# Two held-back steps instead of four, query weights a stage sooner, attention tiles in another order, conditioning sums spread out

## The chip, the cores and the metric

The kernel runs on one core of one Trainium2 chip. The core has a matrix engine (PE in the profile; PEld are its weight loads, which overlap the matmuls), VectorE (DVE), ScalarE (ACT), GpSimd (POOL) and a queue engine (SP) that issues most of the loads from memory; ScalarE issues the stores and a few loads. The metric is the device time of one execution in microseconds (us), the median of several runs.

## The reference

The reference is a two-layer encoder trunk in float32 on one sequence of 1024 rows of width 1024, steered by a conditioning vector `c`.

```
mod = silu(c) @ ada_w[l] + ada_b[l]                  # six vectors of 1024 per layer
h = modulate(rmsnorm(x, g0), shift_m, scale_m)
y = short_conv_mixer(h)                              # layer 0: w_in (1024x3072), 3 taps, gates, w_out
y = mla_mixer(h)                                     # layer 1: 8 heads, low-rank queries, shared low-rank keys and values
x = x + gate_m * rmsnorm(y, g1)
h = modulate(rmsnorm(x, g2), shift_f, scale_f)
y = square(relu(h @ w_up)) @ w_down                  # 1024x4096 and 4096x1024
x = x + gate_f * rmsnorm(y, g3)
```

Before layer 1 the shared keys and values are computed from `x` through a latent of 256 channels, with a norm and a conditioning of their own; queries go through a latent of 384 channels with weights `q_a_w`, then `q_b_w`. Attention is causal by chunks of 64 rows.

## The kernel before, in words

Every matrix product is done in a split form: each float32 operand is written as a high part (a copy by ScalarE) and a low part (a subtraction by VectorE), and three matmuls replace one (`mm`, L155 to L157; `split_w`, L159 to L161). The large products use a seven-product scheme over 2x2 blocks, so that PE does seven block products instead of eight; the sums of blocks are VectorE's.

Loads go through `raw_tile` (L91): four buffers of 512 KB each, shared by all weights, by activations read back from memory and by conditioning matrices. A load is issued when the buffer that it takes has been read.

The order of the instructions on each engine is set by a planner from the dependences and from estimated times; it keeps program order as a priority. Inside `pinned` (L101) the order of the program is kept: for all engines but SP, or for those named.

The stages in order, as far as they are touched:

- *Conditioning.* Each conditioning vector is a list of small steps (`ada_fm`, `ada_bc`, L205 and L241): eight 512 KB loads, each followed by one multiply-add of 128x1024 on VectorE (L187), then a reduction (L218) and a few very small matmuls (L227). The steps wait in a list `bg`, and `run_bg(n)` puts the next n into the program at that point. Each `one(k)` issues the load for k + 1 and then adds k.
- *Convolution* (`conv_phase`): the input projection runs as nine pair jobs (`all_pairs`), each calling `between`, which runs three background steps. `run_bg(99)` stands at its end.
- *Output projections* (`down`, L788): the convolution's and the attention's. Eight rows of 128 channels in chunks of 2, 2 and 4 rows. `fill_row` (L640) splits a row of weights and a row of activations into one slot (`slots_of`); for each chunk PE runs over eight row tiles. In the last chunk each tile goes through `Seam.tile` (L315): square sum on ScalarE, scaling and residual on VectorE, another square sum, the store, and the next norm on ScalarE.
- *Up projection* (`mlp_up`): pairs 0 to 15. `between(i)` runs background steps.
- *Down projection* (`down_pairs`, L646): seven products of eight steps each, in the order 0, 1, 3, 6, 4, 5, 2. A step loads its operands, splits them into rings (four for the one operand, three, later four, for the other) and does 24 matmuls for four row tiles. The last four steps of the last product (`LATE = 4`) are not done in line: their operands are kept, and after the loop each of the four tiles of the second half gets its 24 remaining matmuls and then its `Seam.tile`. The norms of the first half's tiles run meanwhile (`half0`), and `h_steps` (L412) transposes the normed rows for the next stage: a group is four transposes on PE, two outputs on ScalarE (L424) and one subtraction on VectorE (L430). In the first layer `preps` loads and splits the three query weight tiles, after steps 2, 4 and 6 of the last product.
- *Latents* (`first_latents`, L559): three times 24 matmuls; during the third, the transposes of the second half's rows.
- *Attention*: tiles come from the pool `at`, in the order in which they are first asked for. The arena of slots for the output projection is laid over this pool afterwards; a slot can be filled once every tile under it has been read.

Of the kernel before, what the change touches and what calls it, by code (L numbers as in the profile page):

```python
# [17 lines left out]
P = 128  # L18
# [19 lines left out]
PAIRS = D_FF // P // 2  # L38
LATE = 4
RMS = math.sqrt(D)  # L40
# [9 lines left out]
def trunk_kernel(ctx: ExitStack, tc: tile.TileContext, x, c, ada_w, ada_b, norm_g, conv_in_w, conv_w,  # L50
# [300 lines left out]
    def quarter_steps(ys, key, ops):  # L351


        s1, sh = vtile["s" + key], vtile["h" + key]
        kept = [quarter_tile(kk, F32) for kk in range(4)]
        pairs = {}

        def turned(dst, k, half):
            p_ = tp_ps()
            for t in range(4):  # L360
                nc.tensor.transpose(p_[:, t * P:(t + 1) * P], ys[half * 4 + t][:, k * P:(k + 1) * P], ident)
            nc.scalar.activation(dst, p_, AF.Identity, scale=s1[:, k:k + 1], bias=sh[:, k:k + 1])
# [283 lines left out]
    def down_pairs(ys, wd, before, seam, key=None, preps=()):  # L646

        r1, r2, r3, l1 = pool("r1", "right"), pool("r2", "right"), pool("r3", "right"), pool("l1")
        n = PAIRS // 2
        w4 = wd.rearrange("(q two p) d -> p q two d", two=2, p=P)  # L650
        ws = {b: {} for b in ("11", "12", "22")}
# [46 lines left out]
        def half0(i):  # L698

            if i in (3, 5, 7, 9):  # L700
                seam.ahead = 1
                seam.tile((i - 3) // 2, None, [])
            with pinned():
                if i in (0, 2, 4, 6, 8, 10):
                    seam.flush()
                    early(i // 2)
                if i > 10:
                    seam.back()
                    seam.front(steps, 1)
            if i in (n + 2, n + 4, n + 6) and preps:  # L710
                preps.pop(0)(up)

        with pinned([mybir.EngineType.SP]):
            for which, one, more, b, make, done in (
# [11 lines left out]
                if which == 5:  # L726
                    l1.release()
                    xp = pool("xp")
                elif which == 2:
                    r3.release()  # L730
                    r4 = pool("r4", "right")
                    pbs.append(ring(r4))
                    if key:
                        h0 = pool("h0")
                        dst = tuple(h0.tile([P, KD, HALF], F32R, name=nm("h0")) for _ in range(2))
                        up = pool("up")
                        steps = h_steps(tp, ys, 0, key, dst, bank_ps, True)
                for i in range(n):
# [19 lines left out]
                    if which == 5:  # L758
                        half0(i)
                    if which == 2 and i >= n - LATE:  # L760
                        half0(n + i)
                        late.append((pa, pb))
                        continue
# [9 lines left out]
            for t in range(4):  # L773
                with pinned([mybir.EngineType.PE]):
                    for j, (pa, pb) in enumerate(late):
                        products(banks_[t], t, pa, pb, False, j == LATE - 1, True)
                    seam.tile(4 + t, lambda: done(t, banks_[t]), [])
# [10 lines left out]
    def down(slots, sizes, wd, src_fn, ys, seam, steps, per_chunk_bg, before_last=None):  # L788
# [4 lines left out]
        for n_rows in sizes:  # L793
# [9 lines left out]
            for t in range(NT):  # L803
# [10 lines left out]
                else:  # L814
                    nc.vector.tensor_tensor(ys[t], ys[t], p_, op=ALU.add)

    def from_dram(hd):
# [23 lines left out]
    def conv_phase():  # L841
# [213 lines left out]
        for step in all_pairs(up, ops, [job for j in range(1, 4) for job in triple(j)])[::-1]:  # L1055
            step()
        run_bg(99)
        up.release()
# [24 lines left out]
    def mlp_up(l, up, ops, firsts, per_pair_bg):  # L1083
# [32 lines left out]
        def between(i):  # L1116
            flush()
            if i >= AHEAD:
                run_bg(per_pair_bg)
# [128 lines left out]

    h1.release()
    up.release()  # L1250
    h0.release()
    xp.release()
# [9 lines left out]
    def part(pl, tag, bufs, shape):  # L1262
        return tuple(pl.tile(shape, F32R, tag=tag + "hl"[i], name=nm(tag), bufs=bufs) for i in range(2))

    def kv_weights(raw):
# [219 lines left out]
    bg += ada_bc(ad, "g1f", w1, 5 * D, ada_b[1:2, 5 * D:6 * D], norm_g[1, 3:4, :])  # L1485
    last = mlp_up(1, up, hs, firsts, 1)
    ys = [row_tile() for _ in range(NT)]
# [43 lines left out]
```

## Time and profile before

| | us |
|---|---|
| median of 3 runs | 2171.38 (2169.84 to 2172.59) |
| the profiled execution: its time | 2170.84 |
| its span, from first to last instruction | 2169.1 |
| PE busy in it | 2068.5 (95%) |
| VectorE busy | 1542.0 (71%) |
| ScalarE busy | 1083.7 (50%) |
| mean clock granted to PE | 0.988 of full speed |
| read from memory, written | 258.94 MB, 83.89 MB |

A profile line of the timeline reads: start, duration, engine, line of the kernel, operation, output and inputs, shapes, count, and in brackets how long the engine was idle before and what ended that. "PE" lines give each matmul's latency, which overlaps the next; the pace is read from a long run of them. A window line gives, for a stretch, the busy time of each engine with the instructions in it, then the granted clock of PE, the busy share of the transfer engines and the rate in GB/s.

### The profile page before, as it was taken

To read this page: it belongs to the slowest core of one execution; us is meant where nothing else is said; L and a number is where in the kernel's file an instruction comes from. 1 tells how busy PE (TensorE), PEld (TensorE's weight loads), DVE (VectorE), ACT (ScalarE), POOL (GpSimd) and SP (SyncE) were. 2 spreads that over 40 slices of the span, in tenths; PEclk is the share of its full clock that TensorE was granted. 3 is DMA by queue.
4 is the path that set the end of the run, shared out by engine and by line. 5 is a ranking of instruction groups with operands and counts; after the bars stand their busy time and mean duration, and the time that the engine had idled before them with its cause. 6 is when DMAs were issued, how large, how long until landed. Compare 5 with 4: busy or idle time off the path is not lost.

```text
span 2169.1 us, 25064 instructions
## 1 busy us (share of the span) xinstructions
PE 2068.5 (95%) x9438; PEld 1690.3 (78%) x9438; DVE 1542.0 (71%) x2087; ACT 1083.7 (50%) x1533; POOL 5.3 (0%) x13
## 2 busy tenths in 40 slices
PE   4999999889999999998999999989899999999998
PEld 3788878678888788886777888878678888788886
DVE  6877866877655669877688887665876665566576
ACT  4533353735554444455665655564744454544443
POOL 0000000000000000000000000000000000000000
PEclk9999999999999999998999999999999999999999
DMA  7344464256444889546213331043255553774355
GB/s 227 112 140 146 137 200 143 85 195 206 152 146 141 285 289 327 191 152 216 87 50 123 94 104 36 29 156 127 77 194 185 189 170 121 268 247 164 96 174 172
DMA packets 251023, 344.47 MB, mean 159 GB/s; under 512 B 19253, under 2 KB 142482, under 8 KB 250902
## 3 DMA queue, kind: packets, MB, share of 16 engines
q1 hardware_dynamic: 208408, 252.50, 37.0%
q10 hardware_dynamic: 42494, 90.38, 11.2%
q8 instruction: 74, 1.21, 0.2%
q14 instruction: 47, 0.39, 0.1%
HBM read 258.94 MB, written 83.89 MB: 158 GB/s over the span
## 4 chain that ended last, share of the span: by engine, by line
PE 75%; DVE 13%; ACT 6%; DMA 4%; issue 2%; ACTq 0%; SPq 0%; DVEq 0%
PE one L157 41%; PE mm L157 19%; PE tp L157 7%; PE big L157 4%; PE big L1334 2%; ACT junk L272 2%; DMA raw<-in_ada_w_dram 1%; DVE y L328 1%; PE tp L1360 1%; DVE raw L329 1%; DVE acc L187 1%; DMA raw<-ha 1%; DVE av L889 1%; ACT z L1192 1%; DMA aw<-in_ada_w_dram 1%
## 5 line engine op out<-in xcount | busy, mean ns | idle before, releaser
L157 PE MATMUL one<-slot,uphi 128*128 128x512 f32 x1224 | 377.8, 390 | 0.0
L157 PEld LDWEIGHTS one<-slot,uphi 128*128 128x128 f32 x1224 | 230.4, 188 | 48.1 <-issue 0.5
L157 PE MATMUL one<-ring,ring 128*128 128x512 f32 x1152 | 263.0, 390 | 2.3 <-DVE ring L161 2.3
L157 PEld LDWEIGHTS one<-ring,ring 128*128 128x128 f32 x1152 | 215.8, 188 | 48.4 <-ACT ring L160 3.1
L157 PE MATMUL one<-slot,uplo 128*128 128x512 f32 x612 | 240.9, 394 | 8.6 <-DVE y L516 3.8
L161 DVE TENSOR_TENSOR uplo<-raw,uphi 128x1024 fp32r<-128x1024 f32 x127 | 153.2, 1221 | 131.2 <-ACT uphi L160 131.2
L161 DVE TENSOR_TENSOR ring<-raw,ring 128x1024 fp32r<-128x1024 f32 x144 | 174.2, 1219 | 55.8 <-ACT ring L160 55.4
L160 ACT ACTIVATE ring<-raw 128x1024 fp32r<-128x1024 f32 x144 | 149.5, 1051 | 110.6 <-DMA raw<-ha 60.2
L157 PE MATMUL mm<-ring,ring 128*128 128x512 f32 x768 | 189.3, 396 | 7.0 <-DVE ring L161 7.0
L160 ACT ACTIVATE uphi<-raw 128x1024 fp32r<-128x1024 f32 x127 | 134.5, 1060 | 113.0 <-PE one L157 82.1
L157 PE MATMUL big<-slot 128*128 128x512 f32 x768 | 178.9, 393 | 5.3 <-DVE slot L161 4.5
L157 PE MATMUL tp<-ring,ring 128*128 128x512 f32 x768 | 183.9, 389 | 0.0
L160 ACT ACTIVATE ring<-w 128x1024 fp32r<-128x1024 f32 x80 | 84.8, 1060 | 186.0 <-PE tp L157 95.7
L157 PEld LDWEIGHTS mm<-ring,ring 128*128 128x128 f32 x768 | 146.3, 191 | 39.8 <-DVE ring L161 6.0
L157 PEld LDWEIGHTS big<-slot 128*128 128x128 f32 x768 | 144.5, 189 | 36.5 <-DVE slot L161 5.2
L157 PEld LDWEIGHTS tp<-ring,ring 128*128 128x128 f32 x768 | 144.0, 188 | 29.8
L161 DVE TENSOR_TENSOR ring<-w,ring 128x1024 fp32r<-128x1024 f32 x80 | 97.7, 1221 | 88.5 <-ACT ring L160 87.9
L157 PEld LDWEIGHTS one<-slot,uplo 128*128 128x128 f32 x612 | 115.3, 188 | 36.8 <-DVE y L516 5.5
L187 DVE SCALAR_TENSOR_TENSOR acc<-raw,csil,acc 128x1024 f32<-128x1024 f32 x88 | 112.5, 1279 | 27.6 <-DMA raw<-in_ada_w_dram 23.1
L514 ACT ACTIVATE y<-one 128x512 f32<-128x512 f32 x66 | 39.0, 592 | 165.0 <-PE one L157 111.3
L157 PE MATMUL mm<-slot,uphi 128*128 128x512 f32 x344 | 108.7, 398 | 9.5 <-DVE slot L386 9.3
L157 PE MATMUL one<-slot,s 128*128 128x512 f32 x468 | 114.5, 394 | 3.3 <-DVE s L161 3.3
(268 smaller groups left out, 3464.9 us busy)
## 6 DMA issues: line engine op xcount, KB each, us to landing
ha<-y ACTq DMA_DIRECT2D x224, 256.0 KB, 4.1
raw<-ha SPq DMA_DIRECT2D x112, 512.0 KB, 4.0
raw<-in_ada_w_dram SPq DMA_DIRECT2D x80, 512.0 KB, 4.0
raw<-in_mlp_up_w_dram SPq DMA_DIRECT2D x70, 512.0 KB, 4.2
w<-in_mlp_down_w_dram SPq DMA_DIRECT2D x48, 512.0 KB, 6.8
raw<-in_mlp_down_w_dram SPq DMA_DIRECT2D x32, 512.0 KB, 4.7
raw<-in_conv_in_w_dram SPq DMA_DIRECT2D x18, 512.0 KB, 4.0
xs<-raw ACTq DMA_DIRECT2D x18, 512.0 KB, 2.6
```

Of the source, the lines that this page charges most:

```text
L157: nc.tensor.matmul(out_, lhs[a], rhs[b], start=first and i == 0, stop=last and i == 2, skip_group_check=more)
L160: nc.scalar.activation(hi, src, AF.Copy)
L161: nc.vector.tensor_tensor(lo, src, hi.bitcast(F32), op=ALU.subtract)
L187: nc.vector.scalar_tensor_tensor(acc, raw, s, acc, op0=ALU.mult, op1=ALU.add)
L272: nc.scalar.activation(junk, src, AF.Square, accum_out=ss)
L328: nc.vector.scalar_tensor_tensor(y, y, rroot(ss), self.gmb, op0=ALU.mult, op1=ALU.mult)
L329: nc.vector.tensor_tensor(xr, xr, y, op=ALU.add)
L514: nc.scalar.activation(dst, x_, AF.Copy)
L889: nc.vector.scalar_tensor_tensor(acc, raw[:, i, :], csil[:, i:i + 1], acc, op0=ALU.mult, op1=ALU.add)
L1192: nc.scalar.activation(y[32 * i:32 * i + 32, :], p_[32 * j:32 * j + 32, :], AF.Copy, scale=scale)
L1334: nc.tensor.matmul(o_, a, m_, start=j == 0, stop=j == 4)
L1360: nc.tensor.transpose(p_[:, c:c + P], pts[4 * hf + i][:, j * P:(j + 1) * P], ident)
```

## The change

Five edits, none of which changes what is computed:

1. `LATE = 4` becomes `n_late`, two in the first layer's down projection, four in the second's. The transposed groups come two a step, after steps 3, 4 and 5 of the last product, and none after steps 6 and 7; two remain for the tiles after the loop.
2. The query weights are loaded and split in steps 0 to 2 of the product before (`which == 5`). For this the pool `up` is made before `h0` and lies where the weights of block "12" were, beside `xp`.
3. The call that drains the conditioning steps at the end of the convolution is gone; in `down` one step follows each tile of the chunks before the last. The two vectors are looked up where they are used.
4. In the up projections the steps begin at pair 8 instead of pair 4; in the second layer they come two a pair instead of one.
5. In the pool `at` the tiles of key weights, query weights and one rotary scratch tile are asked for first, so that they lie lowest, after the sine table.

```diff
-LATE = 4
@@ quarter_steps
-        s1, sh = vtile["s" + key], vtile["h" + key]
         def turned(dst, k, half):
+            s1, sh = vtile["s" + key], vtile["h" + key]
@@ down_pairs
+        n_late = 2 if key else 4
...
                 if i > 10:
                     seam.back()
-                    seam.front(steps, 1)
-            if i in (n + 2, n + 4, n + 6) and preps:
+                    seam.front(steps, 2 if i < 2 * n - n_late else 0)
+            if i < 3 and preps:
                 preps.pop(0)(up)
...
                 if which == 5:
                     l1.release()
                     xp = pool("xp")
+                    if key:
+                        up = pool("up")
...
                         dst = tuple(h0.tile([P, KD, HALF], F32R, name=nm("h0")) for _ in range(2))
-                        up = pool("up")
...
-                    if which == 2 and i >= n - LATE:
+                    if which == 2 and i >= n - n_late:
...
-                        products(banks_[t], t, pa, pb, False, j == LATE - 1, True)
+                        products(banks_[t], t, pa, pb, False, j == n_late - 1, True)
@@ down
                     nc.vector.tensor_tensor(ys[t], ys[t], p_, op=ALU.add)
+                if f < nf:
+                    run_bg(1)
@@ conv_phase
-        run_bg(99)
@@ mlp_up
-            if i >= AHEAD:
+            if i >= 2 * AHEAD:
                 run_bg(per_pair_bg)
@@ latents and attention
     h1.release()
+    h0.release()
     up.release()
-    h0.release()
...
+    for shape, tags in (([P, 2, HALF], ("kwh", "kwl")), ([P, 3, 256], ("qwh", "qwl")), ([P, HALF], ("zb",))):
+        for tag in tags:
+            at.tile(shape, F32 if tag == "zb" else F32R, tag=tag, name=nm(tag), bufs=1)
...
-    last = mlp_up(1, up, hs, firsts, 1)
+    last = mlp_up(1, up, hs, firsts, 2)
```

## The prediction

> **What bounds the kernel now.** I read four views in this order: the page's totals, the waits of PE (the matrix engine), a table of short windows around the long waits with the clock granted to PE, and the timeline there, engine by engine.
>
> ```profile
> span 2169.1 us, 25064 instructions
> PE 2068.5 (95%) x9438; PEld 1690.3 (78%) x9438; DVE 1542.0 (71%) x2087; ACT 1083.7 (50%) x1533; POOL 5.3 (0%) x13
> ```
>
> PE is busy for 2068.5 of 2169.1 us, so an edit that moves work on other engines can win only what lies in the other 100.6 us, and what PE loses just after a wait by running slowly. The columns below are the total, the number of waits and the longest.
>
> ```profile
> PE mm L157 <- DVE slot L386: 9.3, 4, 3.3
> PE mm L157 <- DVE ring L161: 7.0, 4, 3.1
> PE big L157 <- DVE slot L161: 4.5, 1, 4.5
> PE one L157 <- DVE s L161: 3.3, 3, 2.9
> PE one L421 <- ACT tt L424: 2.7, 1, 2.7
> PE one L157 <- DVE uplo L161: 0.4, 1, 0.4
> ```
>
> The change touches the places of the last five. The first belongs to the first pairs of the up projection, where nothing is edited. What surrounds the others is in these windows (PE busy, PEld, DVE, ACT, POOL, then the PE clock, the DMA share and GB/s), and the last line is a long undisturbed run of matmuls from the chain of waits.
>
> ```profile
> 278.50:282.36 3.86, 0.97 (x9) 0.86 (x7) 3.86 (x7) 2.12 (x3) 0.00 (x0) 1.00 0.55 149
> 282.36:286.80 4.44, 4.44 (x12) 3.52 (x13) 4.43 (x9) 1.57 (x2) 0.00 (x0) 0.62 0.90 300
> 1009.30:1014.30 5.00, 4.99 (x16) 3.83 (x16) 2.43 (x3) 5.00 (x7) 0.00 (x0) 0.66 0.83 268
> 1017.40:1023.50 6.10, 3.27 (x6) 1.78 (x6) 5.70 (x6) 2.33 (x3) 0.00 (x0) 0.50 0.78 272
> 1429.49:1434.50 5.01, 5.01 (x15) 3.77 (x16) 3.44 (x3) 2.43 (x3) 0.00 (x0) 0.68 0.91 301
> 726.07 82.05 PE one L157 x360
> ```
>
> An undisturbed matmul of 128x512 costs 82.05 / 360 = 0.228 us. After a wait of 2.9 us the next 12 took 4.44 us instead of 2.74: the granted clock was 0.62. So a wait of about 3 us or more costs 1.7 us beyond itself, and removing it returns both.
>
> **The change part by part: (A) the end of the convolution.** The call that drained the list of conditioning steps is gone. The list had 10 + 1 + 24 = 35 steps and nine pair jobs take three each, so eight are left: three accumulations (two of which first issue a 512 KB load), one transposing reduction, three empty steps and the small matmuls. They now run one after each tile in the first chunk of the output projection.
>
> ```profile
> 274.50 1.28 DVE L187 SCALAR_TENSOR_TENSOR acc<-raw,csil,acc 128x1024 f32<-128x1024 f32 x1 [1.73 <-DMA raw<-in_ada_w_dram]
> 275.82 1.25 DVE L218 TRANSPOSE_TENSOR_REDUCE part<-acc 128x32 f32<-128x1024 f32 x1
> 277.56 1.20 DVE L161 TENSOR_TENSOR uplo<-raw,uphi 128x1024 fp32r<-128x1024 f32 x1
> 281.62 0.69 DVE L161 TENSOR_TENSOR s<-raw,s 128x512 fp32r<-128x512 f32 x1
> 278.51 0.96 PE L227 MATMUL mm<-part,sel 128*128 128x16 f32 x8
> 282.36 4.61 PE L157 MATMUL one<-slot,s 128*128 128x512 f32 x12 [2.89 <-DVE s L161]
> ```
>
> VectorE stands in front of its queue waiting for the last conditioning load (1.73 us), adds it (1.28), reduces (1.25), and only then splits the weights whose last product PE wants at 279.5. From the start of that last addition to the weights' split lie 277.56 - 274.50 = 3.1 us; without them the chain to `s`, ready now at 282.3, ends near 278.5 to 279; PE wants it at 278.5, as its 0.96 us of small matmuls have moved too. I leave 0.3 us of wait: A = -(2.89 - 0.3) - (4.44 - 2.74) = -4.3 us. Ends: 0, if the two loads and their additions stay where they are, and -4.6.
>
> Here the Trainium skill weighs differently. "TensorE: Matmul & The Clock Gate", section "What's actually happening", has the clock fall to half only after an idle window of about 3.4 us. By that rule a wait of 2.9 us would cost only itself, and A would be 1.7 us smaller; the row above has 0.62 behind it, and I go by the row.
>
> **(B) Where these steps go.** The work is two loads, up to 5.1 us of VectorE (3 x 1.28 + 1.25) and the 0.96 us of PE, which is only moved.
>
> ```profile
> 298.68:320.40 21.72, 21.63 (x95) 17.56 (x94) 11.45 (x10) 13.54 (x15) 0.00 (x0) 1.00 0.72 247
> ```
>
> The first chunk keeps PE full for 21.7 us while VectorE works 11.45. The two loads go ahead of those of rows 2 and 3 in the load queue, which PE wants only at the end of this chunk. I take 0; without this cover up to 5.1 us would be late.
>
> **(C) Conditioning in the up projections.** The sums start at pair 8 instead of 4, and in the second layer two steps a pair instead of one. The 0.4 us wait (`uplo`) is one place in the first layer, behind such a sum; the same can arise at pair 8 in each layer. I take 0, with ends -0.4 and +0.8.
>
> **(D) The first down projection's tail.** Today the last four steps of the last product are held back and done tile by tile; their steps have no matmuls between them, and PE waits for their operands. Each step needs two 512 KB loads, and the three loads of query weights share the same four buffers.
>
> ```profile
> raw<-in_q_a_w_dram SPq DMA_DIRECT2D x3, 512.0 KB, 4.1
> 939.40:955.80 16.40, 16.40 (x74) 13.56 (x74) 14.52 (x19) 9.77 (x13) 0.00 (x0) 1.00 0.47 158
> 1007.87 0.37 SPq L115 DMA_DIRECT2D raw<-in_q_a_w_dram  x1
> 1009.21 0.37 SPq L115 DMA_DIRECT2D raw<-in_mlp_down_w_dram  x1
> 1017.29 0.37 SPq L115 DMA_DIRECT2D raw<-ha  x1
> 1004.73 1.91 PE L421 MATMUL one<-cs,y 128*128 128x128 f32 x16
> 1022.23 1.23 DVE L161 TENSOR_TENSOR ring<-raw,ring 128x1024 fp32r<-128x1024 f32 x1 [0.36 <-ACT ring L160]
> 1023.51 2.93 PE L157 MATMUL mm<-ring,ring 128*128 128x512 f32 x6 [2.56 <-DVE ring L161]
> ```
>
> The weights move to the first three steps of the product before. There one load a step is asked for instead of two, VectorE is idle 1.88 us and ScalarE 6.6 us in 16.4, and the operand rings are three steps (16.4 us) ahead of PE. Three times 1.22 us of VectorE and 1.06 us of ScalarE fit partly in the gaps and wholly in that lead: 0. In the last product every load moves up by one, two or three places: the last two, now at 1009.2 and 1017.3, would leave near 1005.6 and 1006.7. The last operand, ready now at 1023.4, then comes at 1014 to 1018.
>
> PE now does two steps more in line. From 1004.7: six groups of four transposes at 1.91 / 4 = 0.48, 48 matmuls, then 12 for the first held-back tile: 1004.7 + 2.9 + 60 x 0.228 = 1021.3, instead of about 1026.4. ScalarE has two splits (2.1 us) and four outputs of 0.67 in each step of 5.5 us, so it keeps up. But what ends last is another chain, the norm that follows each tile.
>
> ```profile
> 1026.48 0.69 DVE L681 TENSOR_TENSOR y<-y,mm 128x512 f32<-128x512 f32 x1 [3.02 <-PE mm L157]
> 1027.20 1.06 ACT L272 ACTIVATE junk<-y 128x1024 bf16<-128x1024 f32 x1 [5.00 <-DVE y L681]
> 1033.24 0.76 ACT L424 ACTIVATE h<-one,v,v 128x512 fp32r<-128x512 f32 x1
> 1034.57 1.05 ACT L272 ACTIVATE junk<-y 128x1024 bf16<-128x1024 f32 x1
> 1055.64 1.15 ACT L312 ACTIVATE y<-raw,small 128x1024 f32<-128x1024 f32 x1 [0.23 <-DVE small L279]
> 1056.91 0.60 PE L421 MATMUL tp<-cs,y 128*128 128x128 f32 x4
> ```
>
> A tile takes 1034.57 - 1027.20 = 7.37 us through ScalarE and VectorE, 1.33 of which (1033.24 to 1034.57) are the two outputs of a transposed group. PE's 12 matmuls a tile take 2.7. From the first addition to the last tile's result are 1055.64 + 1.15 - 1026.48 = 30.3 us, and PE takes up that result at once at 1056.91: this chain has no slack today. After the change it begins near 1021.5 and is one group (1.33 us) shorter, so it ends at 1021.5 + 30.3 - 1.3 = 1050.5: 6.3 us sooner. PE is there at 1021.3 + 2 x 0.48 + 36 x 0.228 (three tiles) + 51 x 0.228 (latents until the transposes) = 1042.1, and waits 8.4 us: of 14 us that PE gains, the chain keeps more than half. That wait costs the clock again, 1.7 us. D = -6.3 + 1.7 = -4.6 us. Ends: -6.3 with no slow stretch; with operands as late as now (1023.4), the addition comes at 1024.8 and D = -(1.7 + 1.3) + 1.7 = -1.3.
>
> **(F) The end of attention.** The new tile order puts the key and query weights and one scratch tile lowest. The output projection's first slot covers the sine table and mostly those weights, idle throughout the last head; the second still covers queries that the last scores read.
>
> ```profile
> 1425.98 3.90 ACT L160 ACTIVATE slot<-raw 128x1024 fp32r<-128x1024 f32 x4 [0.40 <-ACT o L1395]
> 1427.07 4.63 DVE L161 TENSOR_TENSOR slot<-raw,slot 128x1024 fp32r<-128x1024 f32 x4 [2.68 <-ACT slot L160]
> 1429.49 10.03 PE L157 MATMUL big<-slot 128*128 128x512 f32 x36 [4.54 <-DVE slot L161]
> ```
>
> ```profile
> ACT pt L1363 <- PE tp L1360: 7.7, 9, 2.1
> ACT p L1340 <- DVE small L1337: 4.9, 4, 1.9
> ```
>
> The second fence is what ScalarE waits for in the last head (1396 to 1425). Four splits of each engine stand in a row; PE starts after VectorE's second and needs the fourth (1431.7) three matmuls later. With the first row split early, only two remain and row 1 is ready 4.63 / 2 = 2.3 us sooner. The four early ones go into the last head, whose softmax is a chain over the same engines; I take 0.7 us lost there, as ScalarE is idle 12.6 us there in 13 waits of up to 2.1 us: F = -1.6. Ends: +2.2 (all four, 2.1 + 2.4 = 4.5 us, on the path), and -6.4 if row 1 is early too: 36 matmuls from 1425 would be 8.2 us, so end at 1433.1 instead of 1439.5.
>
> The sum: -4.3 + 0 + 0 - 4.6 - 1.6 = -10.5 us. The profiled execution took 2170.84 us (its span of 2169.1 and 1.7 around it), so 2160.3; the median of the runs is 0.54 above it, so **2161 us**.
>
> **The rivals.**
> 1. *Operands stay late in D.* For it: the splits are slow to be queued, not only slow to land (the last load left at 1017.29, ten microseconds after its neighbours). Against: three loads fewer compete. D = -1.3, time 2164.2.
> 2. *The sums stay where they are*, so A does not do what it says: the planner orders by what is ready, and both loads could still go out early. Against: the projection's four loads now stand ahead of them. A = 0: 2165.2.
> 3. *Row 1 is early too*: F = -6.4, time 2156.1. Against: all four splits today stand behind the last copy of a head's output on ScalarE.
> 4. *Slower: ScalarE takes the transposed groups of step 3 before the split of step 4*, and so on. Then step 4's operand waits for PE's transposes after step 3, and each later step for the one before: 1004.7 + 3.8 (two groups and their outputs) + 3.3 (splits) + 5.5 (matmuls), again 12.6, then 3.8, 5.4 (two splits) and 2.7: the first tile's addition comes near 1042, and the chain ends at 1071 instead of 1056.8, +14.2. With A and F, +8.3: 2179.7. It decides from the point where a group's output stands ahead of the next split. Against it: today the groups come late in ScalarE's queue and the splits pass them.
>
> **How the numbers follow.** The forecast has 0.55, rival 1 0.15, rival 2 0.12, rival 3 0.06, rival 4 0.07; 0.05 is for A = 0, D = -1.3, F = +2.2 and C = +0.8 together, 2173.1. What a measurement can tell from no change is 0.2%, 4.3 us: below 2167.0 or above 2175.7. The forecast and rival 3 are faster, rivals 1 and 2 mostly so: 0.79; same 0.13; slower 0.08. The range goes from all gains at their far ends (-0.4 in C: 2170.84 - 17.7 + 0.5 = 2153.7, and a little beyond) to short of no change: 2152 to 2170.
>
> **What would show it.** A: no `DVE s` wait of 2.9 us and a clock of 1.00 after it; the sums in the output projection's first chunk. D: matmuls without a gap to the first held-back tile, query weight loads beside the product before, then one wait of about 8 us at the latents' transposes for `y`. F: two slot splits inside the last head, the wait for `DVE slot` shorter. Wrong would be: the down projection's steps waiting for rings in line, waits in the first chunk of either projection, or longer softmax waits in the last head.

## The result, and the profile after

| | before | after |
|---|---|---|
| median of 5 runs, us | 2171.38 (2168.59 to 2178.45) | 2162.49 (2161.09 to 2164.95) |
| after / before | | 0.9964, 95% interval 0.9952 to 0.9975 |
| span of the profiled execution, us | 2169.1 | 2161.9 |

The change wins 8.9 us by the medians, 7.8 by the ratio and 7.2 by the two profiled spans; 2161 was predicted. The page's totals of the changed kernel, then PE's waits that answer to those quoted of before (total, number, longest):

```profile
span 2161.9 us, 25072 instructions
PE 2066.3 (96%) x9438; PEld 1690.4 (78%) x9438; DVE 1541.7 (71%) x2087; ACT 1082.9 (50%) x1533; POOL 5.3 (0%) x13
```

```profile
PE mm L156 <- DVE slot L385: 9.3, 4, 3.2
PE tp L420 <- ACT y L311: 5.8, 2, 5.2
...
PE big L156 <- DVE slot L160: 4.5, 1, 4.5
...
PE big L156 <- ACT y L814: 2.2, 2, 1.6
...
PE big L156 <- ACT h L423: 1.4, 1, 1.4
...
PE one L156 <- DVE s L160: 1.1, 3, 0.7
...
PE big L156 <- DVE h L429: 0.9, 1, 0.9
```

(Line numbers shift a little: L157 is now L156, L813 is now L814.) The waits for `ring` in the first down projection's tail (6.0 of the 7.0 us; the other 1.0 is at the very end of the kernel and stays), for `tt` (2.7) and the long one for `s` are gone. Three are new: 5.2 us for `y`, the last normed row, 1.4 for `h`, a transposed group of such rows, and 1.6 for an eviction, the copy of a finished product, which frees its bank (`y` by L814). The wait for the first slot after attention is what it was, 4.5. The timeline of PE at five places, in order of time; the third is the first held-back tile, which now has no wait in front of it:

```profile
279.75 3.01 PE L156 MATMUL one<-slot,s 128*128 128x512 f32 x12 [0.68 <-DVE s L160]
...
309.78 8.54 PE L156 MATMUL big<-slot 128*128 128x512 f32 x36 [1.55 <-ACT y L814]
...
1014.91 2.98 PE L156 MATMUL mm<-ring,ring 128*128 128x512 f32 x12
...
1047.73 0.48 PE L420 MATMUL tp<-cs,y 128*128 128x128 f32 x1 [5.19 <-ACT y L311]
...
1422.47 10.14 PE L156 MATMUL big<-slot 128*128 128x512 f32 x36 [4.54 <-DVE slot L160]
```

The granted clock right behind each wait, in the windows view (PE busy, PEld, DVE, ACT, POOL, PE clock, DMA share, GB/s):

```profile
279.75:282.76 3.01, 3.00 (x13) 2.51 (x14) 3.01 (x4) 0.14 (x1) 0.00 (x0) 1.00 0.85 294
309.78:314.00 4.22, 4.22 (x18) 3.38 (x19) 2.65 (x3) 3.78 (x4) 0.00 (x0) 1.00 0.85 268
1047.73:1052.70 4.97, 4.97 (x16) 4.08 (x17) 2.24 (x4) 1.69 (x3) 0.00 (x0) 0.50 0.01 3
1422.47:1427.50 5.03, 5.03 (x15) 3.75 (x16) 3.44 (x3) 2.01 (x3) 0.00 (x0) 0.66 0.88 294
```

To place the gain, I cut the execution at instructions that every kernel here has, and compare the stretches. They are, in PE's timeline, with the times of before: the eight matmuls `one<-slot,w` that end the startup (84.37); the first `one<-slot,uplo` that waits for L587's `y` (410.81); the last that waits for L516's `y` in the first up projection (468.21, below called the up-pairs cut); the first matmul that waits for `lat`, behind the latents (1080.06); and the first group of transposes that waits for `q`, behind the attention's output projection (1523.47). The edits lie so: 3 in the first stretch, 1 and 2 in the third, 5 in the fourth; edit 4 begins in the second. All the runs told of below are in the table, with the edits that they hold in brackets, so that the stretches which they leave alone show how far one profile differs from another.

| us | convolution and its projection | first up pairs | to the latents | attention and its projection | median | ratio to before (95%) |
|---|---|---|---|---|---|---|
| before | 326.4 | 57.4 | 611.9 | 443.4 | 2171.4 | |
| after | 324.2 | 56.6 | 606.9 | 444.1 | 2162.5 | 0.9964 (0.9952 to 0.9975) |
| tail_alone (1, 2) | 326.3 | 56.6 | 607.3 | 443.9 | 2164.4 | 0.9972 (0.9961 to 0.9982) |
| weights_sooner_alone (2) | 328.0 | 57.9 | 601.6 | 442.8 | 2157.9 | 0.9943 (0.9930 to 0.9955) |
| two_steps_alone (1) | 326.5 | 57.7 | 608.2 | 443.3 | 2166.1 | 0.9983 (0.9973 to 0.9993) |
| sums_alone (3) | 326.0 | 57.8 | 610.5 | 443.5 | 2166.9 | 0.9986 (0.9977 to 0.9995) |
| pair8_alone (4) | 326.4 | 57.7 | 611.3 | 443.0 | 2170.8 | 1.0004 (0.9995 to 1.0013) |
| old_tile_order (all but 5) | 324.1 | 57.0 | 605.6 | 443.7 | 2161.9 | 0.9966 (0.9954 to 0.9979) |
| early_row0 | 324.1 | 56.7 | 607.0 | 445.8 | 2172.6 | 1.0012 (1.0003 to 1.0021) |
| early_row0_moved | 324.1 | 57.1 | 605.6 | 444.9 | 2163.4 | 0.9970 (0.9958 to 0.9981) |
| sums_second_chunk | 322.3 | 57.6 | 605.7 | 444.5 | 2159.8 | 0.9955 (0.9943 to 0.9968) |
| three_held_sums_second | 322.4 | 56.6 | 602.2 | 444.7 | 2156.9 | 0.9939 (0.9927 to 0.9952) |
| four_held_sums_second | 322.4 | 57.8 | 601.5 | 443.2 | 2154.6 | 0.9928 (0.9915 to 0.9940) |
| four_held_row0_pairs | 324.2 | 56.5 | 600.4 | 442.2 | 2156.0 | 0.9934 (0.9920 to 0.9947) |

The startup before the first cut varies by itself between 81.9 and 84.8 us, and a stretch that a kernel leaves alone by up to 1.7. The ratios of the experiments are each to runs of the kernel before on the same chip (medians 2169.7 to 2170.8), so between experiments the ratios compare better than the medians. The parts add up: the ratios of tail_alone, sums_alone and pair8_alone multiply to 0.9962, where the whole change has 0.9964.

### The profile page after: what moved, and what is told of

Its sections match the earlier page's. It is cut to its first block, busy times and chain, and to the rows that moved or that the text cites. A ratio compares the mean times of both kernels' runs of the same rounds, so it can differ in the third digit from the quotient of the medians.

```text
span 2161.9 us, 25072 instructions
## 1 busy us (share of the span) xinstructions
PE 2066.3 (96%) x9438; PEld 1690.4 (78%) x9438; DVE 1541.7 (71%) x2087; ACT 1082.9 (50%) x1533; POOL 5.3 (0%) x13
## 4 chain that ended last, share of the span: by engine, by line
PE 78%; DVE 11%; ACT 6%; DMA 3%; issue 2%; ACTq 0%; SPq 0%; DVEq 0%
PE one L156 42%; PE mm L156 20%; PE tp L156 7%; PE big L156 4%; PE big L1340 2%; ACT junk L271 2%; DVE y L327 1%; PE tp L1366 1%; DVE raw L328 1%; ACT z L1194 1%; DMA aw<-in_ada_w_dram 1%; DMA raw<-hd 1%; PE tp L420 1%; DVE acc L186 1%; DVE av L892 1%
## 5 line engine op out<-in xcount | busy, mean ns | idle before, releaser
L156 PE MATMUL one<-slot,uphi 128*128 128x512 f32 x1224 | 377.6, 389 | 0.0
L156 PEld LDWEIGHTS one<-slot,uphi 128*128 128x128 f32 x1224 | 230.1, 188 | 48.0 <-issue 0.5
L156 PE MATMUL one<-ring,ring 128*128 128x512 f32 x1152 | 262.9, 389 | 2.3 <-DVE ring L160 2.3
L156 PEld LDWEIGHTS one<-ring,ring 128*128 128x128 f32 x1152 | 215.9, 188 | 48.3 <-ACT ring L159 3.1
L156 PE MATMUL one<-slot,uplo 128*128 128x512 f32 x612 | 240.5, 393 | 8.2 <-DVE y L515 3.8
L156 PE MATMUL big<-slot 128*128 128x512 f32 x768 | 179.3, 393 | 6.8 <-DVE slot L160 4.5
L156 PE MATMUL mm<-ring,ring 128*128 128x512 f32 x768 | 184.8, 390 | 1.0 <-DVE ring L160 1.0
L156 PE MATMUL tp<-ring,ring 128*128 128x512 f32 x768 | 183.9, 389 | 0.0
L156 PEld LDWEIGHTS big<-slot 128*128 128x128 f32 x768 | 144.5, 189 | 38.1 <-DVE slot L160 5.2
L156 PEld LDWEIGHTS mm<-ring,ring 128*128 128x128 f32 x768 | 143.7, 188 | 31.2 <-DVE ring L160 1.7
L156 PEld LDWEIGHTS tp<-ring,ring 128*128 128x128 f32 x768 | 144.1, 188 | 29.8
L156 PEld LDWEIGHTS one<-slot,uplo 128*128 128x128 f32 x612 | 115.1, 188 | 35.9 <-DVE y L515 5.5
L156 PE MATMUL mm<-slot,uphi 128*128 128x512 f32 x344 | 108.7, 398 | 9.5 <-DVE slot L385 9.3
L156 PE MATMUL one<-slot,s 128*128 128x512 f32 x468 | 112.8, 390 | 1.1 <-DVE s L160 1.1
```

Source lines behind the costliest of these rows:

```text
L156: nc.tensor.matmul(out_, lhs[a], rhs[b], start=first and i == 0, stop=last and i == 2, skip_group_check=more)
```

## The experiments: the tail of the first down projection

Three kernels, each the one before with a part of the change. *tail_alone* has edits 1 and 2 as they are in the diff. *weights_sooner_alone* has edit 2 alone:

```diff
-            if i in (n + 2, n + 4, n + 6) and preps:
+            if i < 3 and preps:
@@ which == 5
                     xp = pool("xp")
+                    if key:
+                        up = pool("up")
```

*two_steps_alone* has edit 1 alone (`n_late = 2 if key else 4`, groups of transposes two a step).

> The kernel before with edits 1 and 2 alone (two held-back steps, query weights a product sooner). Theory: the gain of the tail does not need the other edits: about -4.6 us against before (-6.2 by the time the last row is normed, 1.6 given back by a slower clock behind the new wait), so 2166 to 2168, with the wait for y of about 5 us at the latents' transposes. Rival: the tail gains only because the convolution's and the up projection's edits shift its loads; alone it gives under 2 us.

> The kernel before with edit 2 alone: query weights loaded and split in the product before, four steps still held back. Theory (both edits are needed): the operands come sooner, but the first held-back tile still needs eight operands without matmuls to cover them; the ring waits of 8.6 us shrink to 3 to 5 us and the time falls by 2 to 4 us. Rival (the three loads were all that was wrong): the ring waits vanish, the first tile's addition comes near 1016 instead of 1026.5, since 24 matmuls a tile start 8 us before the in-line form would, and the gain is 6 to 9 us, more than that of both edits together.

> The kernel before with edit 1 alone: two steps held back, query weights still loaded after steps 2, 4 and 6 of the last product. Theory (both edits are needed): the two steps taken in line now wait for their rings in line, since their loads stand behind the weights' in the four buffers; the gain is 0 to 2 us. Rival (matmuls in line are what matters): the steps cover the loads, the gain is over 4 us.

tail_alone does what was predicted for D: 611.9 to 607.3, -4.6 us, and has the 5.2 us wait for `y`. Its rival falls: the tail needs no other edit.

weights_sooner_alone is the surprise. Alone it wins 12 us by the medians and 10.3 in its stretch, more than the whole change (0.9943 against 0.9964, with intervals that just touch); here the theory fell and the rival held, down to the place of the first addition, though its 6 to 9 us were too few. VectorE's first addition of a held-back tile, and PE's timeline around it, in weights_sooner_alone:

```profile
1015.99 0.69 DVE L681 TENSOR_TENSOR y<-y,mm 128x512 f32<-128x512 f32 x1 [1.99 <-PE mm L157]
```

```profile
1006.50 4.35 PE L157 MATMUL mm<-ring,ring 128*128 128x512 f32 x18
1012.40 0.47 PE L157 MATMUL mm<-ring,ring 128*128 128x512 f32 x1 [1.54 <-DVE ring L161]
1013.45 2.50 PE L157 MATMUL mm<-ring,ring 128*128 128x512 f32 x5 [0.57 <-DVE ring L161]
...
1046.38 0.60 PE L421 MATMUL tp<-cs,y 128*128 128x128 f32 x4
```

Of the 8.6 us of waits at the held-back steps (2.67, 3.11, 0.28, 2.56 before), 2.3 are left. The addition stands at 1015.99 instead of 1026.48, and at 1046.38 PE takes up the last normed row with no wait at all. In the changed kernel, with the same loads but two steps in line, the addition comes at 1018.18 in an execution that is 2.4 us ahead at the up-pairs cut, and PE reaches the row early and waits.

two_steps_alone gains 3.6 us in its stretch, between the theory's 0 to 2 and the rival's over 4: its loads of query weights still stand between the others, yet PE waits 0.58 us for one ring only. So each edit repairs the same thing by itself, the late operands: edit 2 takes the competing loads and their splits away (which of the two counts was not separated), edit 1 puts 48 matmuls in front of them. They are not needed together, and edit 1 costs something that edit 2 does not.

What it costs follows when the time of the first addition is set against the end of the stretch. Both columns are differences of times in one profile: the addition (L681) less the up-pairs cut, and the cut behind the latents less the addition.

| us | held back | query weights | first addition after the up-pairs cut | from there to the cut behind the latents |
|---|---|---|---|---|
| before | 4 | late | 558.3 | 53.6 |
| two_steps_alone | 2 | late | 554.0 | 54.2 |
| tail_alone | 2 | sooner | 553.3 | 53.9 |
| after | 2 | sooner | 552.6 | 54.3 |
| three_held_sums_second | 3 | sooner | 547.8 | 54.4 |
| weights_sooner_alone | 4 | sooner | 548.0 | 53.5 |
| four_held_sums_second | 4 | sooner | 547.8 | 53.6 |

From the first addition on, every kernel takes 53.5 to 54.4 us: the chain of four norms, about 30 us, and what follows it. PE has less work than that in this stretch when two or three steps are held back (it waits), and just enough when four are. So the end is set by when the first addition comes, and holding back *more* than two steps brings it forward: a step in line is 24 matmuls (5.5 us) ahead of it, a held-back step only six (1.4 us), as long as the operands are there.

Two runs test that with the other repair (below) in them. *four_held_sums_second* is the changed kernel with four steps held back again; *three_held_sums_second* holds back three:

```diff
-        n_late = 2 if key else 4
+        n_late = 4
-                    seam.front(steps, 2 if i < 2 * n - n_late else 0)
+                    seam.front(steps, 1)
```

> The changed kernel with two things altered: four steps held back again in the first down projection (query weights stay a product sooner), and the leftover conditioning steps in the second chunk only. Theory: the gains of the runs before add up. With four held back the first tile's addition comes near 1016 instead of 1024 of the changed kernel's own clock and PE reaches the last normed row just as it is ready, so the wait for y and the slow stretch behind it go: 5 us on top of the 2.7 us of the second chunk, 2154 to 2155.5. Rival: they overlap, since both free the same four load buffers; 2157 to 2159.

> As the run before, but three steps held back (the transposed groups two and three a step). Theory: the end is set by the first tile's addition plus 30 us of norms; taking one step in line costs PE 5.5 us before it and saves 1.4 in the tile, but the operand waits of 2.1 us go with it, so the addition comes 1 to 2 us later than with four, PE waits 4 to 5 us for y and loses part of its clock: 1.5 to 3.5 us slower than with four, 2156 to 2158. Rival: the number of held-back steps does not matter once the query weights are out of the way: within 0.5 us of the run before.

The first was met: 2154.63 us, 5.2 below *sums_second_chunk*, the same kernel with two steps held back. The gains add up. It is the fastest by its median, 0.9928 of the kernel before, where the change as made has 0.9964. Its timeline of PE has no wait for `y`:

```profile
1008.16 0.47 PE L156 MATMUL mm<-ring,ring 128*128 128x512 f32 x1 [1.57 <-DVE ring L160]
1009.20 2.50 PE L156 MATMUL mm<-ring,ring 128*128 128x512 f32 x5 [0.57 <-DVE ring L160]
...
1035.47 0.74 PE L156 MATMUL big<-h,uphi 128*128 128x512 f32 x2 [0.56 <-DVE h L429]
...
1042.22 0.60 PE L420 MATMUL tp<-cs,y 128*128 128x128 f32 x4
```

With three held back the addition comes not later, as I had it, but at the same time (547.8 in both rows): the 4.1 us that the step in line costs are about what the ring waits (2.1) and the slow matmuls around them had cost, which are gone. PE then waits further on, for a transposed group that stands behind the norms on ScalarE:

```profile
1031.05 0.79 PE L156 MATMUL big<-h,uplo 128*128 128x512 f32 x1 [3.94 <-ACT h L423]
1032.45 1.22 PE L156 MATMUL big<-h,uphi 128*128 128x512 f32 x2 [0.60 <-DVE h L429]
```

The stretch is 0.75 us longer than with four, the median 2.3 us higher, but the profiled span is 0.4 us lower and the intervals overlap: whether three or four is better is not settled. That two is worse than four is: the intervals of 0.9955 and 0.9928 do not meet. Against three, the stretch of two is 3.5 us longer, but the intervals overlap.

## The experiments: the conditioning sums

*sums_alone* is the kernel before with edit 3 alone. *sums_second_chunk* is the changed kernel with the leftover steps in the second chunk only:

```diff
-                if f < nf:
+                if sizes[0] < f < nf:
                     run_bg(1)
```

> The kernel before with edit 3 alone: the eight leftover conditioning steps in the first output projection. Theory: the wait for s at the end of the convolution goes (-4.3 us with its slow stretch), and a wait of about 1.6 us comes in the first chunk of the projection, behind an eviction that stands in ScalarE's queue after a split which waits for a late load; net -2 to -3 us, 2168.5 to 2169.5. Rival: that new wait belongs to other edits; then -4.3 us, about 2167.

> The changed kernel, but the eight leftover conditioning steps run only in the second chunk of the first output projection, so that their two loads leave after those of rows 2 and 3. Theory: rows 2 and 3 then arrive as before the change, the wait of PE for an eviction in the first chunk (1.55 us and what the clock loses behind it) is gone and no other takes its place: -1.5 to -3.5 us against the changed kernel, 2159 to 2161. Rival: PE waits for late rows or for the eviction wherever the two loads go (the wait moves to the second chunk): no difference, 2162.5.

Both theories were met in the trace. In the first chunk PE waits for an eviction, and the wait is in sums_alone too, so it belongs to edit 3. It comes about, in the changed kernel, by a chain over three queues. The loads on SP, then ScalarE:

```profile
279.73 0.33 SPq L114 DMA_DIRECT2D raw<-hd  x1
281.46 2.60 SPq L114 DMA_DIRECT2D raw<-in_ada_w_dram  x2
284.97 0.65 SPq L114 DMA_DIRECT2D raw<-in_conv_out_w_dram  x1
```

```profile
306.49 1.06 ACT L159 ACTIVATE slot<-raw 128x1024 fp32r<-128x1024 f32 x1 [2.27 <-DMA raw<-in_conv_out_w_dram]
307.76 1.06 ACT L159 ACTIVATE slot<-raw 128x1024 fp32r<-128x1024 f32 x1 [0.21 <-DMA raw<-hd]
308.72 1.01 ACT L814 ACTIVATE y<-big 128x1024 f32<-128x1024 f32 x1
```

The two conditioning loads are issued between those of the rows, and take two of the four load buffers. A row's weights then come late; the split that waits for them (2.27 us) stands ahead of the eviction in ScalarE's queue; and PE, which wants only the bank that this eviction frees, waits 1.55 us. It wants nothing of the late row itself. In sums_alone the same wait is 1.80 us, and there the clock falls behind it:

```profile
308.39 10.08 PE L157 MATMUL big<-slot 128*128 128x512 f32 x36 [1.80 <-ACT y L813]
```

```profile
308.39:312.90 4.51, 4.51 (x13) 3.55 (x14) 2.65 (x3) 2.75 (x3) 0.00 (x0) 0.62 0.90 268
```

The same 36 matmuls take 8.54 us in the changed kernel, at a clock of 1.00, so the new wait cost 1.80 + 1.5 = 3.3 us there and ate most of what the end of the convolution gained: the stretch is 0.4 us shorter than before, where the changed kernel's is 2.2 shorter. This one execution, 2169.67 us, is the slowest of the eleven of sums_alone. Their median is 3.1 us below the kernel before, which by itself does not tell the theory's 2 to 3 from the rival's 4.3; it is the trace that decides. With the steps in the second chunk it is 4.2 shorter, the whole of A, and PE waits for no eviction there: the rival of sums_second_chunk falls. The median is 2.7 us below the changed kernel's; by the two ratios it is 2 us, with intervals that overlap.

*pair8_alone* is the kernel before with edit 4 alone.

> The kernel before with edit 4 alone: conditioning sums from pair 8 of the up projections. Theory: the wait for uplo of 0.39 us at 477.5 and about 0.7 us of small waits in the first pairs go: -0.4 to -1.1 us, 2169 to 2170, no more than a measurement can tell from nothing. Rival: bunched sums (two a pair in the second layer) make new waits late in the second up projection, +0.5 to +1 us.

Nothing that can be measured: 1.0004 (0.9995 to 1.0013). The wait for `uplo` of 0.39 us is gone and the stretch around it is 0.6 shorter, no more than stretches vary by. The "small waits in the first pairs" of my theory were not edit 4's: the second column of the table goes from 56.5 to 57.9 in no relation to it. The new waits of the rival, late in the second layer, did not come.

## The experiments: the end of attention

*old_tile_order* is the changed kernel without edit 5.

> The changed kernel without edit 5 (attention tiles in the old order). Theory: edit 5 moves no instruction, since the splits stand behind the last output copy with it and without it: 2162.5, within 0.1 percent, and the wait for slot is 4.5 us in both. Rival: edit 5 gained its 1.6 us somewhere else, and this kernel is at 2164.

The theory held: 2161.9 against 2162.5, and the wait for the slot is 4.54 us in both. Edit 5 is worth nothing that can be measured, and the trace of after says why. ScalarE, at the end of the last head:

```profile
1417.97 0.60 ACT L1401 ACTIVATE o<-mm 128x512 f32<-128x512 f32 x1 [1.05 <-PE mm L156]
1418.60 0.33 ACTq L1402 DMA_DIRECT2D hd<-o  x1
1418.97 3.90 ACT L159 ACTIVATE slot<-raw 128x1024 fp32r<-128x1024 f32 x4 [0.40 <-ACT o L1401]
```

All four splits stand behind the last copy of a head's output, as before. In the program's table of addresses the first slot lies over the sine table, key weights and query weights, all last read by the start of the last head (the last matmuls on the key and query weights start at 1386.4 and 1388.4), so the memory had been free for some 29 us. To see whether the order was the cause, *early_row0* drops edit 5 and makes that slot before the attention, with the key and query weights inside it:

```diff
+    slot0 = tb.tile([P, 4, D], F32R, name="slot")
     stab = tb.tile([P, S], F32, name="stab")
...
-        kw = part(at, "kw", 1, [P, 2, HALF])
+        kw = tuple(slot0[:, i, :].rearrange("p (k m) -> p k m", k=2) for i in (0, 1))
-        qw_ = part(at, "qw", 1, [P, 3, 256])
+        qw_ = tuple(slot0[:, i, :768].rearrange("p (k m) -> p k m", k=3) for i in (2, 3))
...
-    at.release()
-    tb.release()
+    at.release()
```

(The slot and the table are then released with the rest of the arena.) *early_row0_moved* is the same with the table in a pool of its own above the slot, released with `at`.

> The changed kernel without edit 5; in its place the first slot of the attention's output projection is made before the attention, and key and query weights lie in it (their last use is early in the last head). Theory (the slot's pool opened too late in the order; the memory itself was free): the row's two splits of each engine now stand in the queues at the start of the last head, only two a engine remain behind its last output copy, and the wait for slot of 4.54 us shrinks by 1.5 to 2.5 us: 2160 to 2161, as the term F of the prediction had it. Rival 1: the early splits delay the last head's softmax by as much: 2162.5. Rival 2: the wait is set by row 1, third matmul on, so PE starts sooner but waits the same in all: under 0.5 us gained.

> As the run with the first slot made before the attention, but the sine table lies above that slot, so that every later tile has the address that it has in the changed kernel. Theory (the loss of that run was a tile of the second down projection that lay 4 KB off, over a part of the up projection's input read to its end): the wait of 7.6 us at the start of the second down projection is gone, the time is 0.3 to 0.6 us below the changed kernel's, 2161.9 to 2162.2, since PE does six matmuls of row 0 early and then waits 4.5 us for row 1 all the same. Rival: the wait stays, 2172.

The order was the cause: in both, ScalarE splits the first row around the start of the last head, some 30 us before the last output copy. Here in early_row0_moved:

```profile
1386.19 1.05 ACT L159 ACTIVATE slot<-raw 128x1024 fp32r<-128x1024 f32 x1
1388.23 1.05 ACT L159 ACTIVATE slot<-raw 128x1024 fp32r<-128x1024 f32 x1
```

What differs is when the slot was made, and with it where the key and query weights lie, so a tile of a pool that is opened after another is released is not filled before the last tile of the released pool has been taken, in the order that the planner gives. That the planner works by such a rule is inferred from the orders of these kernels; its own reasons were not seen.

But the gain that was predicted from it does not come. PE and ScalarE in early_row0_moved:

```profile
1413.40 0.48 PE L156 MATMUL big<-slot 128*128 128x512 f32 x1
...
1422.03 5.98 PE L156 MATMUL big<-slot 128*128 128x512 f32 x18 [4.54 <-DVE slot L160]
1429.40 2.79 PE L156 MATMUL big<-slot 128*128 128x512 f32 x11 [1.39 <-ACT y L815]
```

```profile
1418.53 3.90 ACT L159 ACTIVATE slot<-raw 128x1024 fp32r<-128x1024 f32 x4 [0.40 <-ACT o L1400]
1424.43 1.06 ACT L159 ACTIVATE slot<-raw 128x1024 fp32r<-128x1024 f32 x1 [2.01 <-DMA raw<-in_attn_o_w_dram]
1427.37 1.06 ACT L159 ACTIVATE slot<-raw 128x1024 fp32r<-128x1024 f32 x1 [1.88 <-DMA raw<-hd]
1428.34 1.01 ACT L815 ACTIVATE y<-big 128x1024 f32<-128x1024 f32 x1
```

PE does six matmuls of the first row among those of the last head, from 1413.40 on, and then waits 4.54 us all the same, now for row 1: its two splits take the time behind the output copy that row 0's two took before. The 1.4 us of the six matmuls are lost again at 1429.40, where an eviction stands behind a split that waits for a load: the same chain as in the convolution's projection. So rival 2 was right here, and for early_row0_moved the stretch is not shorter (444.9 against 444.1).

early_row0 itself lost ten microseconds, in a place that the edit does not touch, the start of the second down projection:

```profile
1853.75 16.53 PE L156 MATMUL one<-ring,ring 128*128 128x512 f32 x62 [7.58 <-DVE ring L160]
```

There the changed kernel waits 1.15 us. SP's first load of weights for that projection, in early_row0:

```profile
1846.20 0.37 SPq L114 DMA_DIRECT2D w<-in_mlp_down_w_dram  x1
```

and in the changed kernel:

```profile
1822.30 0.37 SPq L114 DMA_DIRECT2D w<-in_mlp_down_w_dram  x1
```

In early_row0 it leaves as the last matmul of the up projection (1845.56, 0.61 us long) ends. The table of addresses gave the theory for the second run: with the sine table kept beside the slot, the tiles above it lay 4 KB higher, and one that the up projection reads to its end came to lie under the first weight tile of the down projection, so that tile's load, and all behind it in SP's order, left late. With the table above the slot the addresses are as in the changed kernel, the wait is 1.15 us again, and the time 2163.4. That was the theory, and it held, but for the 0.3 to 0.6 us of gain, which are not there.

*four_held_row0_pairs* puts everything together, and in the first chunk of both output projections takes the products of row 0 for two tiles ahead of those of row 1.

> Everything together: four steps held back, leftover sums in the second chunk, the first slot made before the attention with the table above it, and in the first chunk of each output projection the products of the first row for two tiles ahead of those of the second row. Theory: the twelve matmuls of row 0 (2.7 us) cover part of the 4.5 us wait for row 1: 1.5 to 2.5 us below the first run of this call, 2152 to 2154. Rival: the wait only moves to rows 2 and 3, whose loads land at 1425 to 1431 whatever PE does: within 0.5 us of the first run.

```profile
1415.19 4.34 PE L156 MATMUL big<-slot 128*128 128x512 f32 x12 [3.42 <-DVE slot L160]
1419.80 71.08 PE L156 MATMUL big<-slot 128*128 128x512 f32 x312 [0.27 <-ACT y L830]
```

The wait after attention falls to 3.42 us and its stretch is 1.0 us shorter than in four_held_sums_second, but the convolution's projection, where the same order of products applies, is 1.9 longer. In all 2156.0 us against 2154.6, with intervals that overlap (the profiled span is 2.1 lower): no gain is shown, neither the theory's 1.5 to 2.5 us nor the rival's place within 0.5 us was met, and the two parts were not separated further.

## Why the prediction was right, and where it was not

*What bounds the kernel.* Right: the gains lie in PE's waits and the slow stretches behind them. PE is busy 2.2 us less in the changed kernel with the same matmuls; the rest are waits. That a wait of about 3 us or more also costs some 1.7 us of pace holds in every profile here: after the startup there are 63 waits of 2.48 us or more in the fourteen profiles, and in the 4.5 us behind each of them the granted clock was under 0.7.

*(A) The end of the convolution.* Right in mechanism and size. 0.3 us of wait were left by the prediction; 0.68 remain, at a clock of 1.00, and 12 matmuls take 3.01 us instead of 4.61: by the rows 2.2 + 1.6 = 3.8 us. The stretch is 4.1 to 4.2 us shorter wherever nothing spoils it (sums_second_chunk, three_held_sums_second and four_held_sums_second), against -4.3. Rival 2, that the sums stay where they are, fell.

*(B) Where the sums go.* The step that failed is "I take 0". The prediction looked at VectorE, which had room, and at the load queue, and said that PE wants rows 2 and 3 only at the end of the chunk. That is so, but it left out that ScalarE's queue holds the splits of those rows in front of the evictions of this chunk, which PE needs at once. Cost: 1.55 us in the changed kernel's profile, where the clock stayed at 1.00, and 3.3 in sums_alone's, where it fell; moving the steps wins 1.9 in the stretch. The far end that the prediction gave, 5.1 us of VectorE being late, was another mechanism.

*(C) Conditioning in the up projections.* Right: the 0.39 us wait is gone, nothing took its place, and no run can tell the sum from 0.

*(D) The tail.* Right in mechanism and in size: -4.6 predicted, -4.6 in tail_alone. The changed kernel enters the tail 3.3 us ahead (its first transposes there are at 1001.45 instead of 1004.73) and takes up the last row at 1047.73 instead of 1056.91, so the tail gains 5.9 (6.3 predicted). PE comes early and waits for `y` and `h` 5.8 + 1.4 + 0.9 = 8.1 us (8.4 predicted), of which the 0.9 was there before. Behind the longest the clock is 0.50, and of the 9.2 us of lead 7.5 are left at the cut behind the latents (1072.52): 1.6 lost, 1.7 predicted. Rival 1 and rival 4 fell: there is no gap on PE up to the first held-back tile at 1014.91 and on through the last. What the prediction did not ask is which of the two edits earns it. It took "PE now does two steps more in line" as part of the gain; the runs show that it takes back 4 to 6 us of what the moved loads alone give (605.7 against 601.5 in the stretch with edit 3 mended, 607.3 against 601.6 without the other edits).

*(F) The end of attention.* Wrong: -1.6 predicted, nothing found. The step that failed is "With the first row split early": the bytes were free, but the splits stayed behind the last output copy. And had they gone early, the next step, "row 1 is ready 2.3 us sooner" and PE with it, fails as well, as early_row0_moved shows: PE's wait stays 4.54 us, and the matmuls done early are lost again behind the next late load. Rival 3 asked for more of the same and fell with it.

*The sum.* Predicted -10.5 on the profiled time; the profiled executions differ by -7.2. Of the 3.3 between them, 2.1 are in the first stretch (B, mostly), 2.2 in the fourth (the 1.6 of F, and 0.6 that such stretches vary by) and 0.4 in the startup; the other stretches give 1.4 back, 0.4 of it the `uplo` wait of C. That the median came within 1.5 us of the forecast is partly luck: the profiled execution of before lies 0.5 us under its median and that of after 1.2 us above, which hides 1.7 of the 3.3 us. No run speaks for the slower rival.

## What to carry to other kernels

When a chain of work on other engines follows a product tile by tile, ask first when its first link can start: hold back enough steps that the first tile ends early (three or four here, not two), and rather move the competing loads out of the way than the matmuls in. A load that is put ahead of others was paid for here at the first queue where something urgent stands behind a consumer of those others; look there, not only at whoever wants the data. That memory is free doesn't mean that it will be used sooner: read the order of the queue. After moving a pool look at every later tile that changes its address.

## What the runs showed of the hardware that was not expected

The clock falls behind shorter waits than I had seen, but not every time. The wait for `q` behind the attention's output projection is in all fourteen profiles of the table, 2.24 to 2.31 us long. In the 4.5 us behind it the granted clock was 1.00 in eight of them and 0.62 to 0.67 in six. Here is one of each, first the changed kernel:

```profile
1516.58 1.32 PE L360 MATMUL tp<-cs,y 128*128 128x128 f32 x8 [2.27 <-ACT q L361]
```

```profile
1516.58:1521.00 4.42, 4.40 (x17) 3.45 (x18) 4.32 (x9) 3.66 (x8) 0.00 (x0) 0.67 0.73 237
```

and then pair8_alone, where the wait is as long:

```profile
1521.43 1.33 PE L361 MATMUL tp<-cs,y 128*128 128x128 f32 x8 [2.27 <-ACT q L362]
```

```profile
1521.43:1526.00 4.57, 4.36 (x20) 2.83 (x20) 4.47 (x9) 3.81 (x8) 0.00 (x0) 1.00 0.68 227
```

Shorter waits go either way too. Behind the 1.63 us for `lat` the clock was 1.00 in all fourteen profiles; behind the eviction's 1.55 us it was 1.00 (the window at 309.78), behind its 1.80 us 0.62 (sums_alone, above). In weights_sooner_alone 1.54 and 0.57 us, one matmul apart, are followed by 0.62, while in four_held_row0_pairs 1.55 and 0.57 us at the same place are followed by 1.00. The window in weights_sooner_alone:

```profile
1012.40:1016.90 4.50, 3.93 (x11) 2.99 (x12) 2.51 (x4) 1.07 (x3) 0.00 (x0) 0.62 0.77 199
```

So in these profiles the length of a wait alone decides only from 2.48 us up. Below that the same wait can lose its clock in one execution and not in the next, and what else decides was not found. What is lost hardly depends on the wait: against the same matmuls at 1.00 it is 1.5 us behind 1.80 (10.08 against 8.54 for 36), 1.6 behind 2.89 (4.61 against 3.01 for 12), 1.6 behind 4.54 (10.14 for 36) and 1.6 behind 5.19 (of 9.2 us of lead 7.5 are left). The Trainium skill ("TensorE: Matmul & The Clock Gate", section "What's actually happening") has half clock after an idle window of about 3.4 us and full clock after a busy one as long. Half clock for 3.4 us loses 1.7 us, which is close to what these rows show; that 1.8 or 2.3 us of waiting can be enough is not in that rule, and the measurement decides.
